# Two pairs of gate/up chunks in each second feed-forward stage computed as seven block products

## The chip, the core and the metric

The kernel runs on one core of a Trainium2 chip. The metric is device time of one execution in microseconds (us). The names of the engines in the profile: PE is TensorE (PEld its weight loads), DVE is VectorE, ACT is ScalarE, POOL is GpSimd, SP issues DMAs. On each engine instructions run in the order in which the program was written; engines wait for each other by semaphores.

## What is computed

A decoder trunk of two layers on 256 tokens of width 1024, in float32. Each layer is a half feed-forward step, a mixer (a state-space group beside differential attention), cross attention to 256 memory tokens, and a second half feed-forward step. Only the feed-forward matters here:

```python
def rms_norm(x, gain):
    y = x32 * lax.rsqrt(jnp.mean(x32 * x32, axis=-1, keepdims=True) + EPS)
    return y * gain
def swiglu(x, w_gate, w_up, w_down):
    return (jax.nn.silu(x @ w_gate) * (x @ w_up)) @ w_down
...
    h = h + 0.5 * swiglu(rms_norm(h, ffn2_norm[l]), ffn2_w_gate[l], ffn2_w_up[l], ffn2_w_down[l])
```

The inner width is 2816, cut into 11 chunks of 256 columns. Gate and up columns of a chunk stand side by side, so a chunk is a product of 256 tokens x 1024 by 1024 x 512.

## The kernel before

**Precision.** Every float32 operand of a matmul is split in two parts: `hi` is a copy rounded to TensorE's fast format (ACT, line 264), `lo` is the remainder (DVE, line 227). A product is three matmuls, hi·hi, hi·lo and lo·hi, added in PSUM. The weights are split on the core as they stream in from memory, so each weight costs one ACT and one DVE pass.

**Units.** All weights stream as units of 128 x 1024 numbers (512 KB), in the order that `stream_plan` writes out. A gate/up unit (kind A) is two blocks of the contraction for the 512 columns of one chunk; a chunk has 4 units. A down unit (kind B) is 128 rows by 1024 columns. One unit serves both blocks of 128 tokens (t = 0 and 1), which is 12 matmuls of 512 columns. In what follows that is called a slot. A feed-forward stage has 44 gate/up slots and 22 down slots.

**A plain chunk.** `project` runs the 4 units of a chunk for both token blocks into two PSUM tiles `mm`. For each block, ACT then takes silu of the gate half (`sg`), DVE multiplies by the up half (`g`), PE transposes `g` into a `tp` bank, and ACT and DVE split the transposed chunk into `gT`. Two chunks later (`LAG`) the two down slots of the chunk add it to the accumulators `acc`.

**The order of the work.** The program keeps a clock of its own (`Clock`) with a cost for every instruction, and uses it only to decide in which order instructions are written to the queues. `tick` is called before each three matmuls, four times in a slot: it first calls `feed`, then lets side tasks write whatever the clock says is due (`run_due`), and adds 0.64 us to the planned position `main`. Each unit has a planned position `need`. `feed` writes the split of a unit when its `need` is at most 4.0 us (`LEAD`) ahead of `main`, which is six ticks, one and a half slots, and when one of five buffers (`N_W`) is free. So an evacuation that a side task writes at the end of a slot stands in DVE's queue ahead of the splits for everything that is more than one and a half slots away.

**Gains.** The gain vector of the norm in front of a stage is multiplied into the weights, as the scale of the two split instructions (`split_unit`, halves of 512 columns). The row factor of the norm is applied at the evacuation.

**Seams.** `prep` adds a stage's result to the residual `h`, transposes it and splits it into `xh`, `xl` for the next stage; the first chunk of the next stage runs all of t = 0 before t = 1, to give t = 1 the time.

**Tables.** `ssm_tables(1)`, which prepares constants of layer 1's mixer, runs as a side task during layer 0's second feed-forward stage.

Of the kernel before, what the change touches and what calls it, by code (L numbers as in the profile page):

```python
# [11 lines left out]
F32 = mybir.dt.float32  # L12
# [7 lines left out]
L = 2  # L20
D = 1024
# [24 lines left out]
START = (22.0, 34.0)  # L46


def rel_bucket(n):
# [26 lines left out]
def stream_plan():  # L76

    plan = []
    for l in range(L):
        def ffn(nm):  # L80
            for j in range(NCH):
                for kp in range(4):
                    plan.append((nm + "_gu", l, 4 * j + kp, "A", (nm, l, 2 * kp), 4 if j == 0 and len(plan) >= 4 else 1))
                if j >= LAG:
                    for f in range(2):
                        plan.append((nm + "_dn", l, 2 * (j - LAG) + f, "B", None, 1))
            for n in range(2 * (NCH - LAG), 2 * NCH):
                plan.append((nm + "_dn", l, n, "B", None, 2 * LAG))

        def chunk(nm, c, norm, skew):  # L90
# [17 lines left out]
        ffn("ffn2")  # L108
# [210 lines left out]
class Trunk:  # L319
    def __init__(self, ctx, tc, io):  # L320
        self.tc, self.io = tc, io
        self.c = Clock(tc.nc)
        self.v, self.a, self.g, self.p = Vector(self.c), Scalar(self.c), Pool(self.c), Tensor(self.c)
        P = lambda name, bufs, **kw: ctx.enter_context(tc.tile_pool(name=name, bufs=bufs, **kw))
        self.const = P("const", 1)
        self.xp = P("xp", 2)
        self.rawp = P("raw", N_RAW)
        self.hip = P("hi", N_W)
        self.lop = P("lo", N_W)
        self.tab = P("tab", 1)  # L330
# [9 lines left out]
        self.tp = P("tp", 2, space=bass.MemoryType.PSUM)  # L340
# [4 lines left out]
        self.raw, self.w = {}, {}  # L345
# [14 lines left out]
        return self.sm.tile([128, n], F32, tag=f"{name}{n}", name=name)  # L360

    def tpt(self):
        p = self.tp.tile([128, 512], F32, tag="tp", name="tp")
        self.tpown[id(p)] = (p, len(self.tpfree))
        self.tpfree.append(math.inf)
        return p

    def tp_done(self, p):
# [1 line left out]

    def tp_wait(self):

        while self.tpfree[-2] + TPW > self.c.now:
            yield max(self.c.now + 0.01, min(self.tpfree[-2] + TPW, self.c.now + 0.3))

    def mmt(self):
        c = self.c
# [37 lines left out]
    def split(self, hi, lo, src):  # L415
        self.a.activation(hi, src, AF.Copy)
        self.v.tensor_tensor(lo, src, hi.bitcast(F32), op=ALU.subtract)

    def rstd(self, r, ssq, n, wd):
        self.g.tensor_scalar(r, ssq, 1.0 / wd, EPS, op0=ALU.mult, op1=ALU.add)  # L420
        self.g.tensor_tensor(r, r, self.mhalf[:, 0:n], op=ALU.pow)
# [16 lines left out]
    def feed(self, least=-1):  # L438

        c = self.c  # L440
        prev, c.cur = c.cur, self.stream
        n = len(self.plan)
        while self.nsplit < 2 * n:
            u, q = divmod(self.nsplit, 2)
            if u >= self.nfree + N_W or (u > least and self.need[u] + q * STEP / 2 > self.main + LEAD):
                break
            self.split_next()
        c.cur = prev

    def split_next(self):  # L450
        u, q = divmod(self.nsplit, 2)
        self.load_to(u + 1)
        self.split_unit(u, q)
        self.nsplit += 1
        self.load_to(u + N_RAW + q)

    def load_to(self, m):
        while self.nload < min(m, len(self.plan)):
            r = self.rawp.tile([128, 1024], F32, tag="raw", name="raw")
            self.tc.nc.sync.dma_start(r, self.io["wst"][self.nload])  # L460
            self.raw[self.nload] = r
            self.nload += 1

    def split_unit(self, i, q):
        kind, gain = self.plan[i][3:5]
# [186 lines left out]
        return out  # L652


    def prep(self, t, acc, coef):
        h = self.h[t]
        t0 = []
        for n in range(2):
            s = slice(512 * n, 512 * n + 512)
            self.v.scalar_tensor_tensor(h[:, s], acc[n], coef, h[:, s], op0=ALU.mult, op1=ALU.add)  # L660
            t0.append(self.c.cur.t)
        self.acc_done()
        x = self.xt()
        for n in range(2):
            self.c.cur.t = t0[n]
            yield
            yield from self.tp_wait()
            p = self.transpose4(h, [512 * n + 128 * i for i in range(4)])
            o = [a[:, 4 * n:4 * n + 4, :].rearrange("p a b -> p (a b)") for a in x]
            self.split(o[0], o[1], p)  # L670
            self.tp_done(p)
        self.x[t] = x
        with self.c.aside():
            self.row_stat(t)
# [56 lines left out]
    def ffn(self, nm, preps, tail):  # L731
# [53 lines left out]
                    self.free_unit()  # L785
        for i in range(NCH - LAG, NCH):
            self.c.wait(*tasks[i])
        base = NCH - LAG
        return self.blocks(nm + "_dn", accs, lambda t, k: xs(base + k // 2, k % 2, t), 2 * LAG, False, True, tail)

# [651 lines left out]
    def setup(self):  # L1442
# [7 lines left out]
        self.nload = 2  # L1450
# [80 lines left out]
    def run(self):  # L1531
        c = self.c
        self.setup()
        preps = None
        prep = lambda coef: (lambda t, acc: self.prep(t, acc, coef))
        tb = {}
        tables = [c.spawn(self.ssm_tables(0, tb), START[0]), c.spawn(self.setup_rest(), START[1])]
        for l in range(L):
            preps = self.ffn("ffn1", preps, prep(0.5))
            preps = self.mixer(l, preps, tb, tables, prep(1.0))  # L1540
            preps = self.cross(l, preps, prep(1.0))
# [6 lines left out]
            preps = self.ffn("ffn2", preps, prep(0.5) if l < L - 1 else (lambda t, acc: self.final(t, acc, 0.5)))  # L1548
        c.wait(*preps)
        c.drain()  # L1550
        assert self.upos == len(self.plan) == self.nfree
# [9 lines left out]
def lay_out(a):  # L1561
# [11 lines left out]
    for l in range(L):  # L1573
# [11 lines left out]
    wst = np.concatenate([groups[s, l][n:n + 1] for s, l, n, _, _, _ in stream_plan()[0]], axis=0)  # L1585
    col = lambda v: v.reshape(-1, 128).T
    gains = np.concatenate(
        [col(f[k][l]) for l in range(L)
# [30 lines left out]
```

## Time and profile before

| what | value |
|---|---|
| median of 3 runs | 1214.55 us (1214.17 to 1214.58) |
| the profiled execution | 1216.16 us, of which the span shown is 1214.3 us |
| PE busy | 1198.7 us (99%) |
| DVE busy | 831.3 us (68%) |
| ACT busy | 701.5 us (58%) |
| granted TensorE clock | 0.999 of full speed |
| second feed-forward of layer 0 | 422.6 to 619.8 us of the span |
| second feed-forward of layer 1 | 1020.3 us to the end |

The profile gives busy time of each engine, the same in 40 slices, the chain of waits that ended last, and groups of like instructions with their number, busy time, mean duration, and the idle time in front of them with what ended it. A view of waits lists who waited for whom, in total, in number, and the longest. The timeline lists instructions in order: start, length, engine, line, operation, output<-inputs, and in brackets the idle time before. Matmuls overlap, so their cost is read from one start to the next.

### The profile page before, as it was taken

Reading aid. Unit: us, or ns where it says so; the run is one execution under the profiler, and the core shown is the slowest. Engines: PE = TensorE matmul, PEld = TensorE weight load, DVE = VectorE, ACT = ScalarE, POOL = GpSimd, SP = SyncE. Lnnn points to the kernel's source line nnn. Section 1 sums busy time; section 2 is a strip of 40 time slices with the busy share of each in tenths; the row PEclk is TensorE's granted clock in tenths of the full one; section 3 lists DMA queues with packets and bytes.
Section 4 is the critical chain, followed back from the end, with each engine's and each line's share of the span. In section 5 each row is a group of like instructions: output and inputs, shape, how many; then the busy total and the mean of one; then the engine's idle time right before and its main releaser. Section 6 shows DMA issues by size and latency. Waiting matters only on the chain.

```text
span 1214.3 us, 17886 instructions
## 1 busy us (share of the span) xinstructions
PE 1198.7 (99%) x6628; PEld 979.9 (81%) x6628; DVE 831.3 (68%) x1502; ACT 701.5 (58%) x1270; POOL 45.1 (4%) x104
## 2 busy tenths in 40 slices
PE   9999999999999999999999999999999999999997
PEld 7888878777888888887888888887678888888886
DVE  5797777497767668777665655565977675655564
ACT  6665455667767555644565554465686665644553
POOL 2100001000000010000100000000000000000000
PEclk9999999999999999999999999999999999999999
DMA  8656556544644465655656555555346445655652
GB/s 281 214 181 191 163 163 188 155 138 123 208 156 138 144 209 184 190 157 158 187 176 218 169 180 192 191 168 162 122 140 209 138 146 166 199 182 191 208 181 79
DMA packets 59975, 210.92 MB, mean 174 GB/s; under 512 B 7168, under 2 KB 8288, under 8 KB 59888
## 3 DMA queue, kind: packets, MB, share of 16 engines
q1 hardware_dynamic: 56304, 202.92, 52.2%
q0 software_dynamic: 2000, 5.24, 1.5%
q10 hardware_dynamic: 1584, 1.62, 0.5%
q8 instruction: 52, 0.85, 0.3%
q14 instruction: 35, 0.29, 0.1%
HBM read 207.00 MB, written 1.05 MB: 171 GB/s over the span
## 4 chain that ended last, share of the span: by engine, by line
PE 93%; DVE 2%; ACT 2%; DMA 1%; issue 1%; ACTq 0%; POOLq 0%; POOL 0%; DVEq 0%
PE mm L303 54%; PE acc L303 32%; PE tp L314 5%; PE tp L303 1%; DMA uq<-z 1%; DVE wlo L227 1%; DVE p L227 1%; ACT junk L264 0%; DMA h<-in_x 0%; ACT whi L264 0%; ACT z L264 0%; DVE nm L227 0%; DVE yT L227 0%; ACT yg L264 0%; ACT up L264 0%
## 5 line engine op out<-in xcount | busy, mean ns | idle before, releaser
L227 DVE SCALAR_TENSOR_TENSOR wlo<-raw,gains,whi 128x512 fp32r<-128x512 f32 x544 | 383.8, 746 | 96.9 <-ACT whi L264 92.5
L264 ACT ACTIVATE whi<-raw,gains 128x512 fp32r<-128x512 f32 x544 | 353.7, 713 | 14.2 <-DMA raw<-in_wst 7.0
L303 PE MATMUL mm<-whi,xh 128*128 128x512 f32 x896 | 356.5, 398 | 0.0
L303 PE MATMUL mm<-whi,xl 128*128 128x512 f32 x896 | 349.8, 390 | 0.0
L303 PE MATMUL mm<-wlo,xh 128*128 128x512 f32 x896 | 349.3, 390 | 0.3 <-DVE wlo L227 0.3
L303 PE MATMUL acc<-whi,gT 128*128 128x512 f32 (+1 forms) x712 | 239.7, 399 | 0.0
L303 PEld LDWEIGHTS mm<-whi,xh 128*128 128x128 f32 x896 | 168.6, 188 | 36.3 <-issue 1.3
L303 PEld LDWEIGHTS mm<-whi,xl 128*128 128x128 f32 x896 | 168.5, 188 | 35.6
L303 PEld LDWEIGHTS mm<-wlo,xh 128*128 128x128 f32 x896 | 168.8, 188 | 33.0 <-DVE wlo L227 0.6
L227 DVE TENSOR_TENSOR wlo<-raw,whi 128x512 fp32r<-128x512 f32 x224 | 147.3, 686 | 37.3 <-ACT whi L264 35.7
L264 ACT ACTIVATE whi<-raw 128x512 fp32r<-128x512 f32 x224 | 130.6, 624 | 59.8 <-DMA raw<-in_wst 42.7
L303 PEld LDWEIGHTS acc<-whi,gT 128*128 128x128 f32 x712 | 133.3, 188 | 25.8
L264 ACT ACTIVATE sg<-mm,rstd 128x256 f32<-128x256 f32 x88 | 41.8, 475 | 190.3 <-PE mm L303 190.1
L303 PE MATMUL acc<-wlo,gT 128*128 128x512 f32 (+1 forms) x356 | 138.2, 388 | 0.0
L227 DVE SCALAR_TENSOR_TENSOR g<-mm,rstd,sg 128x256 f32<-128x256 f32 x88 | 42.4, 482 | 129.0 <-ACT sg L264 128.5
L303 PE MATMUL mm<-whi,mem 128*128 128x512 f32 x256 | 92.6, 410 | 0.0
L303 PEld LDWEIGHTS acc<-wlo,gT 128*128 128x128 f32 x356 | 67.2, 189 | 11.0
L264 ACT ACTIVATE xh<-tp 128x512 fp32r<-128x512 f32 x40 | 23.9, 598 | 77.8 <-PE tp L314 77.8
L303 PEld LDWEIGHTS mm<-whi,mem 128*128 128x128 f32 x256 | 48.1, 188 | 11.5 <-issue 1.3
L303 PE MATMUL mm<-wlo,mem 128*128 128x512 f32 x128 | 51.0, 398 | 3.5 <-DVE wlo L227 3.5
L227 DVE TENSOR_TENSOR xl<-tp,xh 128x512 fp32r<-128x512 f32 x40 | 27.6, 689 | 31.7 <-ACT xh L264 31.7
L264 ACT ACTIVATE gT<-tp 128x512 fp32r<-128x512 f32 x44 | 26.3, 599 | 36.7 <-PE tp L314 36.7
(214 smaller groups left out, 1093.6 us busy)
## 6 DMA issues: line engine op xcount, KB each, us to landing
raw<-in_wst SPq DMA_DIRECT2D x382, 512.0 KB, 4.2
raw<-in_wst SPq DMA_DIRECT2D x4, 256.0 KB, 5.1
mem<-in_mem POOLq DMA_DIRECT2D x2, 512.0 KB, 6.3
uq<-z ACTq DMA_DIRECT2D x8, 128.0 KB, 4.8
bglu<-in_b_glu POOLq DMA_DIRECT2D x2, 512.0 KB, 3.8
h<-in_x SPq DMA_DIRECT2D x3, 256.0 KB, 5.7
bc<-in_s5b POOLq DMA_DIRECT2D x2, 256.0 KB, 3.0
bc<-in_s5c POOLq DMA_DIRECT2D x2, 256.0 KB, 3.1
```

The source lines that it names most:

```text
L227: r = getattr(self.e, name)(*a, **k)
L264: r = self.e.activation(out, in_, func, **k)
L303: r = self.e.matmul(out, lhsT, rhs, **k)
L314: r = self.e.transpose(out, in_, ident)
```

## The change

Chunks 2 and 3, and chunks 7 and 8, of both second feed-forward stages are each computed as a 2 x 2 block product with seven block products instead of eight (Strassen's scheme in Winograd's form). The blocks of the left side are two token blocks by two halves of the contraction, those of the right side two halves of the contraction by two chunks. A block product (`block`) is 2 units of 6 matmuls each into one `tp` bank, one slot in all. Each pair of chunks takes seven such steps.

- The left side: `combos` adds `xh` and `xl` back together, forms four sums of blocks on DVE and splits these once per stage.
- The right side: four weight blocks of 2 units each are loaded, X, Y, P and Q. A step's operand is split when it is due; four of the seven steps first add another block to it on DVE (`split_whole`: add, then ACT's `hi`, then DVE's `lo`, for each of the 2 units).
- The results: three products are copied out by ACT; `sums`, `c11`, `c12` and `c21` put the four results together on DVE, and silu, multiplication, transposition and the split to `gT` follow as before.
- The order of the stage is written out in `SECOND`: P and D are slots of plain gate/up chunks and of down units, S2 and S7 are steps of the two pairs. For reference the slots behind P0 and P1 (eight slots) are numbered 1 to 52 in the order of that string, so that pair 2's seven steps are slots 1, 5, 8, 12, 15, 19, 22 and pair 7's are 26, 29, 33, 36, 40, 43, 46. The steps that add are the third, fourth, sixth and seventh of each pair.
- In these stages the gain is multiplied into `xh` and `xl` at the seam (`split_gain`, four pieces of 128 columns instead of one of 512), and a plain weight unit is split in one piece of 1024 columns instead of two of 512.
- The two `tp` banks are handed out by which is free first instead of in turn, and `ssm_tables(1)` moves to the first feed-forward stage of layer 1.

```diff
+SECOND = (
+    "P0 P0 P0 P0 P1 P1 P1 P1 "
+    "S2 P4 D0 P4 S2 D0 P4 S2 P4 D1 P5 S2 D1 P5 S2 P5 D4 P5 S2 D4 P6 S2 P6 D5 P6 "
+    "S7 D3 P6 S7 D3 D5 P9 S7 P9 D2 S7 D2 P9 D6 S7 P9 D6 S7 P10 P10 S7 P10 P10 D8 D8 D7 D7"
+)
+PAIR = (
+    ("Q3", (1, 1), "X", "X", None),
+    ("Q1", (0, 0), "P", "P", None),
+    ("Q7", (1, 0), "Y", "X", "Y"),
+    ("Q6", None, None, "X", "P"),
+    ("Q2", (0, 1), "Q", "Q", None),
+    ("Q5", None, None, "Y", "P"),
+    ("Q4", None, None, "X", "Q"),
+)
...
-        at += 2 * STEP * n
+        at += STEP if plan[i][3] == "S" else 2 * STEP * n
...
+    def split_gain(self, x, n, src, nm, l):
...
+        for g, b in zip(gc, blk):
+            self.copy(o[0][:, b], src[:, b], scale=g)
...
+            self.v.scalar_tensor_tensor(o[1][:, b], src[:, b], g, o[0][:, b].bitcast(F32), op0=ALU.mult, op1=ALU.subtract)
...
+    def split_whole(self, i):
...
+        if kind == "S":
+            pair, u, _, operand, add = op
+            r = self.blk[pair, operand, u]
+            if add is not None:
+                self.v.tensor_tensor(r, r, self.blk[pair, add, u], op=ALU.add)
+        else:
+            r = self.raw.pop(i)
+        self.split(hi, lo, r)
...
+        def block(ps, name):
+            xh, xl = E[name]
+            for u in range(2):
+                w = self.unit(nm + "_gu")
+                for i in range(2):
+                    self.tick(w[2 + i])
+                    s = slice(512 * i, 512 * i + 512)
+                    k = 2 * u + i
+                    self.p.matmul(ps, xh[:, k, :], w[0][:, s], start=k == 0, stop=False)
+                    self.p.matmul(ps, xh[:, k, :], w[1][:, s], start=False, stop=False)
+                    self.p.matmul(ps, xl[:, k, :], w[0][:, s], start=False, stop=k == 3)
+                self.free_unit()
...
+            def sums():
+                yield st["q1"]
+                v.tensor_tensor(u2, ps, q1, op=ALU.add)
...
+                v.tensor_tensor(u3, u3, u2, op=ALU.add)
...
+                v.tensor_tensor(q3, q3, u2, op=ALU.subtract)
+            def c11():
+                yield st["u"]
+                v.tensor_tensor(q1, ps, q1, op=ALU.add)
+                self.tp_done(ps)
+                yield
+                swiglu(q1, q1, 0)
+            def c12():
+                yield st["u"]
+                v.scalar_tensor_tensor(u2, ps, -1.0, u3, op0=ALU.mult, op1=ALU.subtract)
+                v.tensor_tensor(q3, q3, ps, op=ALU.subtract)
...
+                swiglu(u2, u2, 1)
+                swiglu(q3, q3, 0)
...
         for l in range(L):
+            if l:
+                tb = {}
+                tables = [c.spawn(self.ssm_tables(l, tb), c.now + 12.0)]
...
-            if l < L - 1:
-                tb = {}
-                tables = [c.spawn(self.ssm_tables(l + 1, tb), c.now + 10.0)]
```

More of the change, by code (lines that the diff above doesn't have):

```diff
@@ L46, with second_items @@
 START = (22.0, 34.0)
+SECOND = (
[3 rows of a table added]
+)
[8 more added lines that the diff above has]
+)
+def second_items():
+    seen = {}
+    for item in SECOND.split():
+        k = seen[item] = seen.get(item, -1) + 1
+        yield item[0], int(item[1:]), k
 def rel_bucket(n):
@@ L88, in ffn, with second @@
                 plan.append((nm + "_dn", l, n, "B", None, 2 * LAG))
+        def second(nm):
+            for kind, j, k in second_items():
+                if kind == "P":
+                    plan.append((nm + "_gu", l, 4 * j + k, "A", None, 4 if j == 0 else 1))
+                elif kind == "D":
+                    plan.append((nm + "_dn", l, 2 * j + k, "B", None, 1))
+                else:
+                    _, block, to, operand, add = PAIR[k]
+                    for u in range(2):
+                        n = None if block is None else 4 * (j + block[0]) + 2 * block[1] + u
+                        plan.append((nm + "_gu", l, n, "S", ((l, j), u, to, operand, add), 1))
+            for n in range(2 * (NCH - LAG), 2 * NCH):
+                plan.append((nm + "_dn", l, n, "B", None, 2 * LAG))
         def chunk(nm, c, norm, skew):
@@ L107, in stream_plan @@
             plan.append(("wo", l, k, "B", None, 4))
-        ffn("ffn2")
+        second("ffn2")
     need, at, i = [], 0.0, 0
@@ L371, in tp_wait, with tp_main @@
     def tp_wait(self):
-        while self.tpfree[-2] + TPW > self.c.now:
-            yield max(self.c.now + 0.01, min(self.tpfree[-2] + TPW, self.c.now + 0.3))
+        while min(self.tpfree) + TPW > self.c.now:
+            yield max(self.c.now + 0.01, min(min(self.tpfree) + TPW, self.c.now + 0.3))
+    def tp_main(self):
+        c = self.c
+        while min(self.tpfree) == math.inf or (c.heap and c.heap[0][0] + TPW <= min(self.tpfree) > c.now + TPW):
+            c.step_idle()
+        return self.tpt()
     def mmt(self):
@@ L417, in split @@
         self.v.tensor_tensor(lo, src, hi.bitcast(F32), op=ALU.subtract)
+    def split_gain(self, x, n, src, nm, l):
+        g0 = l * NGAIN + GOFF[nm] + 4 * n
+        gc = [self.gains[:, g0 + i:g0 + i + 1] for i in range(4)]
+        blk = [slice(128 * i, 128 * i + 128) for i in range(4)]
+        o = [a[:, 4 * n:4 * n + 4, :].rearrange("p a b -> p (a b)") for a in x]
+        for g, b in zip(gc, blk):
+            self.copy(o[0][:, b], src[:, b], scale=g)
+        t = self.c.cur.t
+        self.c.cur.t -= 0.6
+        for g, b in zip(gc, blk):
+            self.v.scalar_tensor_tensor(o[1][:, b], src[:, b], g, o[0][:, b].bitcast(F32), op0=ALU.mult, op1=ALU.subtract)
+        self.c.cur.t = max(self.c.cur.t, t)
     def rstd(self, r, ssq, n, wd):
@@ L652, in blocks, with prep @@
         return out
-    def prep(self, t, acc, coef):
+    def prep(self, t, acc, coef, gain=None):
         h = self.h[t]
@@ L668, in prep @@
             p = self.transpose4(h, [512 * n + 128 * i for i in range(4)])
-            o = [a[:, 4 * n:4 * n + 4, :].rearrange("p a b -> p (a b)") for a in x]
-            self.split(o[0], o[1], p)
+            if gain is not None:
+                self.split_gain(x, n, p, *gain)
+            else:
+                o = [a[:, 4 * n:4 * n + 4, :].rearrange("p a b -> p (a b)") for a in x]
+                self.split(o[0], o[1], p)
             self.tp_done(p)
@@ new lines, in ffn_second, with swiglu, to_columns, parts @@
+    def ffn_second(self, nm, preps, tail):
+        c, v = self.c, self.v
+        gT, bank, accs, tasks = {}, {}, None, {}
+        E = {}
+        def swiglu(ps, o, t):
+            c.cur.t = max(c.cur.t, self.rt[t])
+            self.a.activation(o[:, 0:256], ps[:, 0:256], AF.Silu, scale=self.r[t])
+            v.scalar_tensor_tensor(o[:, 256:512], ps[:, 256:512], self.r[t], o[:, 0:256], op0=ALU.mult, op1=ALU.mult)
+        def to_columns(p, g, t):
+            for f in range(2):
+                o = f * 256 + t * 128
+                self.p.transpose(p[:, o:o + 128], g[:, 256 + f * 128:384 + f * 128], self.ident)
+        def parts(j, p):
+            hl = self.s4t([128, 2, 512], F32R, name="gT")
+            self.split(hl[:, 0, :], hl[:, 1, :], p)
+            self.tp_done(p)
+            gT[j] = hl
+        def evac(j, before):
+            def f(t, ps):
+                if before is not None:
+                    yield before[t]
+                z = self.zp.tile([128, 512], F32, tag="z", name="z")
+                swiglu(ps, z, t)
+                self.mm_done()
+                yield
+                if j not in bank:
+                    yield from self.tp_wait()
+                    bank[j] = self.tpt()
+                    to_columns(bank[j], z, t)
+                else:
+                    to_columns(bank[j], z, t)
+                    parts(j, bank[j])
+            return f
+        def chunk_done(j, g0, g1, *deps):
+            for d in deps:
+                yield d
+            yield from self.tp_wait()
+            p = self.tpt()
+            to_columns(p, g0, 0)
+            to_columns(p, g1, 1)
+            parts(j, p)
+        def block(ps, name):
+            xh, xl = E[name]
+            for u in range(2):
+                w = self.unit(nm + "_gu")
[7 more added lines that the diff above has]
+                self.free_unit()
+        def pair_step(j, k):
+            name = PAIR[k][0]
+            if k == 0:
+                c.wait(combo)
+                st.clear()
+                st["s"] = [self.s4t([128, 2, 512], name="qs") for _ in range(2)]
+            q3, q1, u2, u3 = (x[:, i, :] for x in st["s"] for i in range(2))
+            ps = self.tp_main()
+            block(ps, name)
+            def copied(o):
+                self.copy(o, ps)
+                self.tp_done(ps)
+                return
+                yield
+            def sums():
+                yield st["q1"]
+                v.tensor_tensor(u2, ps, q1, op=ALU.add)
+                self.tp_done(ps)
+                yield st["q7"]
+                v.tensor_tensor(u3, u3, u2, op=ALU.add)
+                yield st["q3"]
+                v.tensor_tensor(q3, q3, u2, op=ALU.subtract)
+            def c11():
+                yield st["u"]
+                v.tensor_tensor(q1, ps, q1, op=ALU.add)
+                self.tp_done(ps)
+                yield
+                swiglu(q1, q1, 0)
[3 more added lines that the diff above has]
+                v.tensor_tensor(q3, q3, ps, op=ALU.subtract)
+                self.tp_done(ps)
+                yield
+                swiglu(u2, u2, 1)
+                swiglu(q3, q3, 0)
+            def c21():
+                yield st["c12"]
+                v.tensor_tensor(u3, ps, u3, op=ALU.add)
+                self.tp_done(ps)
+                yield
+                swiglu(u3, u3, 1)
+            if name == "Q3":
+                st["q3"] = c.spawn(copied(q3))
+            elif name == "Q1":
+                st["q1"] = c.spawn(copied(q1))
+            elif name == "Q7":
+                st["q7"] = c.spawn(copied(u3))
+            elif name == "Q6":
+                st["u"] = c.spawn(sums())
+            elif name == "Q2":
+                st["c11"] = c.spawn(c11())
+            elif name == "Q5":
+                st["c12"] = c.spawn(c12())
+                tasks[j + 1] = [c.spawn(chunk_done(j + 1, q3, u2, st["c12"]))]
+            else:
+                tasks[j] = [c.spawn(chunk_done(j, q1, u3, st["c11"], c.spawn(c21())))]
+        st = {}
+        combo = None
+        def xs(j, f, t):
+            o = f * 256 + t * 128
+            return gT[j][:, 0, o:o + 128], gT[j][:, 1, o:o + 128]
+        before, ps = None, None
+        for kind, j, k in second_items():
+            if kind == "P":
+                if j == 0:
+                    if k == 0:
+                        tasks[0] = self.project(nm + "_gu", self.x, evac(0, None), preps)
+                    if k < 3:
+                        continue
+                    before = tasks[0]
+                    combo = c.spawn(self.combos(E))
+                    continue
+                if k == 0:
+                    ps, tasks[j] = [self.mmt(), self.mmt()], []
+                u = self.unit(nm + "_gu")
+                for t in range(2):
+                    self.mm_a(ps[t], self.x[t], u, 2 * k, k == 0, k == 3)
+                    if k == 3:
+                        tasks[j].append(c.spawn(evac(j, before)(t, ps[t])))
+                self.free_unit()
+                if k == 3:
+                    before = tasks[j]
+            elif kind == "S":
+                pair_step(j, k)
+            else:
+                c.wait(*tasks[j])
+                if accs is None:
+                    accs = [self.acc_main(), self.acc_main()]
+                u = self.unit(nm + "_dn")
+                for t in range(2):
+                    self.mm_b(accs[t], *xs(j, k, t), u, j == 0 and k == 0, False)
+                self.free_unit()
+        for i in range(NCH - LAG, NCH):
+            c.wait(*tasks[i])
```

92 lines of the change are left out of this document (74 added, 18 removed).

## The prediction

> **What bounds the kernel now.** I read the page's first lines, then who TensorE waits for, then the busy time of the feed-forward stages, then TensorE's own pace.
>
> ```profile
> span 1214.3 us, 17886 instructions
> PE 1198.7 (99%) x6628; PEld 979.9 (81%) x6628; DVE 831.3 (68%) x1502; ACT 701.5 (58%) x1270; POOL 45.1 (4%) x104
> ```
>
> The waits of PE (total, times, longest):
>
> ```profile
> PE mm L303 <- DVE wlo L227: 3.8, 5, 1.4
> PE tp L314 <- ACT up L264: 1.9, 2, 1.0
> ```
>
> Three stages: layer 0's second feed-forward, layer 1's first, layer 1's second up to the last split. After the colon pair come length, then busy time of PE, PEld, DVE, ACT, POOL, then the granted clock.
>
> ```profile
> 422.60:619.80 197.20, 197.20 (x1110) 160.91 (x1109) 145.94 (x310) 108.11 (x187) 9.56 (x20) 1.00 0.59 181
> 619.80:806.70 186.90, 186.90 (x854) 153.82 (x853) 111.83 (x174) 99.99 (x174) 1.48 (x4) 1.00 0.56 186
> 1020.30:1206.60 186.30, 186.28 (x857) 153.61 (x855) 111.51 (x175) 99.53 (x173) 1.29 (x3) 1.00 0.53 177
> ```
>
> In these stages PE is never idle. A busy PE need not be at its peak, so I also read its pace:
>
> ```profile
> 463.19 0.39 PE L303 MATMUL mm<-whi,xh 128*128 128x512 f32 x1
> 463.41 0.39 PE L303 MATMUL mm<-wlo,xh 128*128 128x512 f32 x1
> 463.64 0.39 PE L303 MATMUL mm<-whi,xl 128*128 128x512 f32 x1
> 463.87 0.39 PE L303 MATMUL mm<-whi,xh 128*128 128x512 f32 x1
> ```
>
> Four starts span 0.68 us: one matmul per 0.227 us. So the kernel is bound by the number of matmuls, and a removed one gives 0.227 us as long as nothing else becomes late. A slot of 12 takes 2.72 us; with the transposes in it, the stage of 66 slots gives 186.9 / 66 = 2.83 us per slot.
>
> **What is removed.** A pair of chunks takes 8 slots of 12 = 96 matmuls now, and 7 x 12 = 84 after. Twelve less per pair, four pairs: 48 x 0.227 = 10.9 us, 5.45 us per layer. Transposes stay at four per chunk. [...] The trace shows 227 ns here, and 10.9 stands.
>
> **What is added, and on whom.** Durations of the pieces:
>
> ```profile
> L227 DVE SCALAR_TENSOR_TENSOR wlo<-raw,gains,whi 128x512 fp32r<-128x512 f32 x544 | 383.8, 746 | 96.9 <-ACT whi L264 92.5
> L227 DVE TENSOR_TENSOR p<-p 128x1024 f32<-128x1024 f32 x4 | 4.9, 1220 | 0.1
> L264 ACT ACTIVATE up<-uq 128x1024 f32<-128x1024 f32 x2 | 2.1, 1056 | 5.5 <-DMA uq<-z 5.5
> L227 DVE SCALAR_TENSOR_TENSOR g<-mm,rstd,sg 128x256 f32<-128x256 f32 x88 | 42.4, 482 | 129.0 <-ACT sg L264 128.5
> L264 ACT ACTIVATE sg<-mm,rstd 128x256 f32<-128x256 f32 x88 | 41.8, 475 | 190.3 <-PE mm L303 190.1
> L227 DVE TENSOR_TENSOR gT<-tp,gT 128x512 fp32r<-128x512 f32 x44 | 30.3, 690 | 23.8 <-ACT gT L264 23.7
> ```
>
> Two instructions back to back overlap a little:
>
> ```profile
> 521.38 2.35 DVE L227 TENSOR_TENSOR Vt<-pr,bbar 128x1024 f32<-128x1024 f32 x2
> ```
>
> Two of 1.22 us in 2.35: the second starts 1.13 to 1.14 us after the first. So on a busy DVE a pass over 1024 costs 1.14, over 512 0.61 (gT) to 0.60, `g` 0.40.
>
> A plain unit is cheaper than before: one pass of 1.14 on DVE instead of two of 0.75 less the same overlap, and it has no bearing on PE. A step's unit without an add costs the same 1.14, but feeds only 6 matmuls. A unit with an add is the dear one. Its three instructions stand next to each other in the program: DVE adds (1.22), ACT makes `hi` from the sum (1.06), DVE makes `lo` from sum and `hi` (1.14). DVE runs in order, so it stands still while ACT works. What follows an engine starts 0.03 us after it:
>
> ```profile
> 665.18 0.69 DVE L227 TENSOR_TENSOR wlo<-raw,whi 128x512 fp32r<-128x512 f32 x1 [1.13 <-ACT whi L264]
> 670.53 0.48 DVE L227 SCALAR_TENSOR_TENSOR g<-mm,rstd,sg 128x256 f32<-128x256 f32 x1 [4.67 <-ACT sg L264]
> 671.05 0.69 DVE L227 TENSOR_TENSOR wlo<-raw,whi 128x512 fp32r<-128x512 f32 x1
> ```
>
> and on ACT:
>
> ```profile
> 670.03 0.47 ACT L264 ACTIVATE sg<-mm,rstd 128x256 f32<-128x256 f32 x1 [4.88 <-PE mm L303]
> ```
>
> ACT ends at 670.50, DVE starts at 670.53. So one such unit holds DVE for 1.22 + 0.03 + 1.06 + 0.03 + 1.14 = 3.48 us, a step of two units for 6.96, while the step itself takes PE 2.72. There are four such steps in each pair.
>
> These rows show a second thing. DVE stood idle for 4.67 us in front of `g`, with weights left to split: `g` waits for PE's last matmul of the chunk, and the splits behind it in the queue wait too. The planner writes a split six ticks, 1.5 slots, before its use; so whatever is due later than 1.5 slots after such an evacuation can only begin after it. This is how I find the due dates: start from an evacuation that waits for PE, add up DVE's queue from there to the last `lo` of a step, and compare with PE's time to the middle of that step (1.36 us into it, when its second unit starts). Numbers are slots.
>
> *Step 22 (the last of the first pair).* The result of step 15 is evacuated by `c11`, 0.2 us after slot 15 ends (a matmul's 0.39 less 0.227, and the hop). DVE then has: `c11` 0.60, its `g` 0.40, unit 18 1.14, step 19 6.96, unit 20 1.14, two `g` of chunk 5 0.80, unit 21 1.14, `gT` 0.61, the two of `c12` 1.20, step 22 6.96. With the 0.2: 21.15 us. PE gets there in 6 x 2.83 + 1.36 = 18.3. Late by 2.8 us.
>
> *Step 46 (the last of the second pair).* From the end of slot 40: 0.2, `c11` and `g` 1.00, step 43 6.96, two `g` of chunk 9 0.80, unit 44 1.14, `gT` 0.61, unit 45 1.14, `c12` 1.20, step 46 6.96: 20.0 us. PE needs 5 x 2.83 + 1.36 = 15.5. Late by 4.5 us, part of it already at step 43.
>
> *Step 12.* From the end of slot 9, where chunk 4 ends: 0.2, silu 0.50, `g` 0.40, step 12 6.96 = 8.06, with chunk 4's `gT` before its second unit 8.67. PE needs 2 x 2.83 + 1.36 = 7.0. Late by 1.05 to 1.65; I take 1.3.
>
> *Steps 8, 19, 33, 36* come out in time the same way. Step 19: 0.2 + 1.00 + 1.14 + 6.96 = 9.3 of 9.85. Step 36, from the end of slot 28: 0.2 + 0.9 + 0.61 + 4 x 1.14 + 2 x 6.96 = 20.2 of 21.2. In front of step 8 no DVE instruction waits for PE.
>
> *Slot 1.* In the four slots of P1 DVE gets the block sums: two of 1.14, four of 0.60, the first split (0.60 on ACT, then 0.61), besides four units (4.56), a `gT` (0.61) and the evacuation (1.1): 12.2 us against 12.7 to the middle of slot 1. If the other three splits (1.2 each) come ahead it is up to 3 late. I take 0.5, with 0 and 3 as ends.
>
> Per layer 2.8 + 4.5 + 1.3 + 0.5 = 9.1 us of waits, 18.2 in both.
>
> **The rest, at nothing.** At the seam `xh` and `xl` are made in four pieces of 128 columns:
>
> ```profile
> 428.46 0.60 ACT L264 ACTIVATE xh<-tp 128x512 fp32r<-128x512 f32 x1 [0.53 <-PE tp L314]
> 429.09 0.69 DVE L227 TENSOR_TENSOR xl<-tp,xh 128x512 fp32r<-128x512 f32 x1 [0.43 <-ACT xh L264]
> L264 ACT ACTIVATE sb<-sb,nm 128x128 f32<-128x128 f32 x16 | 6.2, 392 | 4.5 <-DVE nm L227 4.4
> L227 DVE SCALAR_TENSOR_TENSOR sb<-sb,sums 128x128 f32<-128x128 f32 x8 | 2.8, 351 | 0.3
> ```
>
> Four of these take about 4 x 0.3 = 1.2 us instead of 0.6 to 0.7, so the second half of t = 1 is ready at some 430.4 instead of 429.8. PE begins t = 1 at 428.95 and wants that half 12 matmuls later, at 431.7. The matmuls of t = 0 cover it; without cover it would be 0.6 us per half. The tables of layer 1 move with all their instructions, their DMAs on POOL's queue too, from the 197.2 us stage to the 186.9 us one: 34 us of DVE into a stage where it has 75 to spare, exactly what the other stage bore without a wait of PE, and the 10 us that they cost PE move along. SP's queue carries 8 loads per pair as before; the steps without a load leave it idle. Of the `tp` banks a step holds one for about 2.7 + 0.8 us, a chunk's transposes the other for two to three, and steps are two slots apart at least: 0, and if a bank is late, below 1 us each time.
>
> **The sum.** The profiled execution took 1216.16 us (its span 1214.3); the runs' median is 1214.55, and what changes adds to either. -10.9 + 18.2 = +7.3: 1221.9 us by the runs. Ends of this case: without the `gT` and one `g` in front, and nothing at slot 1, the waits are 1.8 + 3.5 + 1.05 = 6.35 per layer, +1.8, 1216.4; with `c12`'s two `g` in front of the last unit (0.80 in two places), 1.65 at step 12 and 3 at slot 1 they are 3.6 + 5.3 + 1.65 + 3.0 = 13.55, +16.2, 1230.8.
>
> **Rivals.**
> *DVE's standstill is filled.* If the 1.12 us between add and `lo` hold other due DVE work, or adds run ahead of the evacuations, a step costs 4.56 or less. Step 22 is in time once 0.7 of the 1.12 are filled in its four units, step 46 only when nearly all is; then the 10.9 us stay: 1203.7, or 1204 to 1212 when part does. For it: in the 197.2 us stage DVE was busy for 145.9 and PE still did not wait; and a pair's adds and splits alone are busy for 22 x 1.14 = 25.1 us of the 18 slots (51 us) about it. Against it: add, `hi` and `lo` are written one after the other, and the row at 670.53 shows that nothing overtakes.
> *The waits eat just the gain.* With 4.2 to 6.7 us of waits per layer the result is within 0.2% (2.4 us, about what a measurement can tell): around 1214.5.
> *The clock falls.* The trace opens with TensorE at half pace:
>
> ```profile
> 7.65 0.63 PE L303 MATMUL mm<-whi,xh 128*128 128x512 f32 x1
> 8.08 0.63 PE L303 MATMUL mm<-whi,xl 128*128 128x512 f32 x1
> 8.51 0.63 PE L303 MATMUL mm<-whi,xh 128*128 128x512 f32 x1
> 10.06 0.40 PE L303 MATMUL mm<-whi,xh 128*128 128x512 f32 x1
> 10.30 0.39 PE L303 MATMUL mm<-wlo,xh 128*128 128x512 f32 x1
> ```
>
> It takes 0.43 us per matmul for over 2 us of work, then 0.227. A long wait could bring that state back: 1 us for the 2.2 us seen here, some 4 if the whole slow opening of 9 us counts. With the long waits at steps 22 and 46 in two layers that is 4 to 16 us on top, 1226 to 1238. Against it: before, no wait of 1.4 us did so, and each lateness here is shared by two units with 6 matmuls between. [...]
>
> **Chances.** Forecast 0.54, from the queue's order, which I trust more than its exact sums; standstill filled in good part 0.32, since a queue that runs ahead at some steps would undo the larger terms; even 0.08; clock 0.06. So faster 0.32, same 0.08, slower 0.60. The likeliest case alone spans 1216 to 1231; to hold 8 in 10 the range must take in most of the faster case: 1205 to 1230, which leaves out a full saving and the clock's fall.
>
> **What would show it.** In the profile after: 48 matmuls fewer, at 0.227 us still; among the waits of PE, its step matmuls on DVE's `lo`, some 18 us in all, the longest in steps 22 and 46; on DVE, `lo` of the steps waiting about 1.1 us each for ACT, 32 times. If PE's waits stay below 8 us in all, the due dates are wrong and the change is faster. If PE waits as long but for transposes or banks, the place is wrong.

## The result and the profile after

The changed kernel takes 1235.72 us (median of 4 runs, 1232.87 to 1238.97) against 1214.55 before (also 4 runs): ratio 1.0172, 95% interval 1.0155 to 1.0189. It is slower, as forecast, but by 21.2 us instead of 7.3, and outside the range. The profiled execution took 1238.06 us, its span 1236.3. Lines of `before.py` 227, 264 and 303 are lines 268, 305 and 344 of this kernel.

The first lines of the page, and then the waits of PE (total, times, longest):

```profile
span 1236.3 us, 17726 instructions
PE 1201.5 (97%) x6580; PEld 973.4 (79%) x6580; DVE 904.8 (73%) x1498; ACT 711.1 (58%) x1206; POOL 45.1 (4%) x104
```

```profile
PE tp L344 <- DVE wlo L268: 10.7, 16, 0.8
PE tp L344 <- ACT whi L305: 4.7, 8, 0.9
PE mm L344 <- DVE wlo L268: 4.1, 5, 1.4
PE tp L344 <- ACT eh L305: 2.4, 2, 1.2
```

48 matmuls are gone (6628 to 6580). The 4.1 us that `mm` waits for `wlo` was there before (3.8). New are the waits of `tp`, the bank of the step products, for the splits of the step's weights and of the block sums (`eh`). The three stages again:

```profile
421.90:617.90 196.00, 186.24 (x829) 148.94 (x829) 148.41 (x168) 105.87 (x139) 1.48 (x4) 1.00 0.51 176
617.90:815.00 197.10, 197.10 (x1109) 160.83 (x1108) 146.10 (x310) 106.61 (x186) 9.58 (x20) 1.00 0.58 181
1029.20:1228.60 199.40, 189.77 (x833) 151.93 (x831) 148.25 (x170) 103.99 (x137) 1.90 (x4) 0.97 0.49 164
```

The middle row now carries the tables: 197.1 us, just what the stage that had them took before (197.2), so the move is neutral. A feed-forward stage without tables took 186.9 us before; with 24 matmuls fewer it should take 181.5. The second one of layer 0 takes 196.0, and PE, which had no holes there, is now busy for 186.2 of them.

Where they lie follows from the starts of the matmuls: for each slot, the time from its first start to the next slot's, less 12 x 0.227 and 0.109 per transpose.

| late by (us) | forecast | layer 0 | layer 1 |
|---|---|---|---|
| slot 1 and the transposes ahead of it | 0.5 | 2.98 | 2.94 |
| step 12 | 1.3 | 1.59 | 1.54 |
| step 22 | 2.8 | 3.41 | 5.89 |
| steps 33 and 36 | 0 | 1.75 | 1.73 |
| steps 43 and 46 | 4.5 | 5.08 | 6.59 |
| all | 9.1 | 14.8 | 18.7 |

DVE in front of step 22 of layer 0, in its order, shows the queue that the prediction added up, instruction for instruction (`qs` at 491.69 is `c11`, the two at 504 are `c12`):

```profile
491.69 0.69 DVE L268 TENSOR_TENSOR qs<-tp,qs 128x512 f32<-128x512 f32 x1 [1.11 <-PE tp L344]
492.30 1.22 DVE L268 TENSOR_TENSOR wlo<-raw,whi 128x1024 fp32r<-128x1024 f32 x1
493.44 0.48 DVE L268 SCALAR_TENSOR_TENSOR qs<-qs,rstd 128x256 f32<-128x256 f32 x1
493.83 1.22 DVE L268 TENSOR_TENSOR blkY<-blkY,blkP 128x1024 f32<-128x1024 f32 x1
496.25 1.23 DVE L268 TENSOR_TENSOR wlo<-blkY,whi 128x1024 fp32r<-128x1024 f32 x1 [1.21 <-ACT whi L305]
497.40 1.22 DVE L268 TENSOR_TENSOR blkY<-blkY,blkP 128x1024 f32<-128x1024 f32 x1
499.83 1.23 DVE L268 TENSOR_TENSOR wlo<-blkY,whi 128x1024 fp32r<-128x1024 f32 x1 [1.21 <-ACT whi L305]
...
504.02 0.69 DVE L268 SCALAR_TENSOR_TENSOR qs<-tp,qs 128x512 f32<-128x512 f32 x1
504.62 0.68 DVE L268 TENSOR_TENSOR qs<-qs,tp 128x512 f32<-128x512 f32 x1
505.22 0.68 DVE L268 TENSOR_TENSOR gT<-tp,gT 128x512 fp32r<-128x512 f32 x1
505.82 1.22 DVE L268 TENSOR_TENSOR blkX<-blkX,blkQ 128x1024 f32<-128x1024 f32 x1
508.22 1.23 DVE L268 TENSOR_TENSOR wlo<-blkX,whi 128x1024 fp32r<-128x1024 f32 x1 [1.19 <-ACT whi L305]
```

The bracket in front of each such `wlo` is the standstill: 1.2 us in which DVE waits for ACT's `hi` of the sum that DVE has just made. PE at the same place:

```profile
508.31 0.43 PE L344 MATMUL tp<-whi,xh 128*128 128x512 f32 x1
509.50 0.51 PE L344 MATMUL tp<-wlo,xh 128*128 128x512 f32 x1 [0.76 <-DVE wlo L268]
...
511.79 0.50 PE L344 MATMUL tp<-whi,xh 128*128 128x512 f32 x1 [0.87 <-ACT whi L305]
513.05 0.50 PE L344 MATMUL tp<-wlo,xh 128*128 128x512 f32 x1 [0.76 <-DVE wlo L268]
```

From start to start it loses 0.96 us once and 1.03 twice. Layer 1 has the same waits, and a second loss: in step 22 and step 46 the granted clock falls to half. The window before the fall and the fall itself (third to last column: the clock), then the same at step 46:

```profile
1115.66:1119.07 3.41, 1.81 (x8) 0.96 (x6) 2.23 (x3) 1.21 (x2) 0.00 (x0) 1.00 0.00 0
1119.07:1125.90 6.83, 6.30 (x16) 4.67 (x17) 5.82 (x8) 4.42 (x7) 0.00 (x0) 0.50 0.67 241
1194.17:1197.58 3.41, 1.79 (x7) 0.93 (x6) 2.23 (x5) 3.24 (x5) 0.00 (x0) 1.00 0.00 0
1197.58:1200.99 3.41, 3.41 (x12) 2.72 (x11) 3.11 (x4) 2.05 (x3) 0.00 (x0) 0.50 0.41 94
```

In the first of the two rows with 0.50 matmuls start 0.43 us apart (1124.24, 1124.66, 1125.09) instead of 0.227. The two last 10.24 us, which at half pace costs up to 5.1.

### The profile page after: what moved, and what is told of

Its sections match the earlier page's. It is cut to its first block, busy times and chain, and to the rows that moved or that the text cites. A ratio compares the mean times of both kernels' runs of the same rounds, so it can differ in the third digit from the quotient of the medians.

```text
span 1236.3 us, 17726 instructions
## 1 busy us (share of the span) xinstructions
PE 1201.5 (97%) x6580; PEld 973.4 (79%) x6580; DVE 904.8 (73%) x1498; ACT 711.1 (58%) x1206; POOL 45.1 (4%) x104
## 4 chain that ended last, share of the span: by engine, by line
PE 81%; DVE 11%; ACT 4%; issue 2%; DMA 1%; ACTq 0%; POOLq 0%; POOL 0%; DVEq 0%
PE mm L344 42%; PE acc L344 29%; PE tp L344 6%; PE tp L355 5%; DVE wlo L268 5%; ACT whi L305 3%; DVE blkX L268 2%; DMA uq<-z 1%; DVE blkY L268 1%; DVE qs L268 1%; DVE p L268 1%; DVE gT L268 1%; DMA h<-in_x 0%; DVE z L268 0%; DVE xf L268 0%
## 5 line engine op out<-in xcount | busy, mean ns | idle before, releaser
L268 DVE SCALAR_TENSOR_TENSOR wlo<-raw,gains,whi 128x512 fp32r<-128x512 f32 x368 | 263.1, 747 | 92.9 <-ACT whi L305 91.5
L344 PE MATMUL mm<-whi,xh 128*128 128x512 f32 x768 | 308.0, 401 | 0.0
L344 PE MATMUL mm<-wlo,xh 128*128 128x512 f32 x768 | 300.6, 392 | 0.3 <-DVE wlo L268 0.3
L344 PE MATMUL mm<-whi,xl 128*128 128x512 f32 x768 | 300.8, 392 | 0.0
L305 ACT ACTIVATE whi<-raw,gains 128x512 fp32r<-128x512 f32 x368 | 240.9, 713 | 14.3 <-DMA raw<-in_wst 5.7
L268 DVE TENSOR_TENSOR wlo<-raw,whi 128x512 fp32r<-128x512 f32 (+1 forms) x236 | 209.0, 912 | 29.0 <-ACT whi L305 27.9
L305 ACT ACTIVATE whi<-raw 128x512 fp32r<-128x512 f32 (+1 forms) x236 | 181.0, 805 | 45.6 <-DMA raw<-in_wst 18.9
L305 ACT ACTIVATE whi<-blkX 128x1024 fp32r<-128x1024 f32 x32 | 33.6, 1057 | 55.0 <-DVE blkX L268 55.0
L268 DVE TENSOR_TENSOR wlo<-blkX,whi 128x1024 fp32r<-128x1024 f32 x32 | 39.2, 1225 | 33.7 <-ACT whi L305 33.7
L305 ACT ACTIVATE z<-mm,rstd 128x256 f32<-128x256 f32 (+1 forms) x52 | 29.4, 568 | 39.5 <-PE mm L344 38.9
```

Of the source, the lines that this page charges most:

```text
L268: r = getattr(self.e, name)(*a, **k)
L305: r = self.e.activation(out, in_, func, **k)
L344: r = self.e.matmul(out, lhsT, rhs, **k)
```

## The experiments

State of the question: the theory is that DVE's standstill between add and `lo` makes the queues of the steps too long (with the block sums late at slot 1 as a second cause). Rivals: the sheer amount of work on DVE and ACT, the planner's short lead, the block steps or the other edits themselves.

**Adds together.** The second add fills the time in which ACT makes the first `hi`:

```diff
-            if add is not None:
-                self.v.tensor_tensor(r, r, self.blk[pair, add, u], op=ALU.add)
+            if add is not None and u == 0:
+                for k in range(2):
+                    a = self.blk[pair, operand, k]
+                    self.v.tensor_tensor(a, a, self.blk[pair, add, k], op=ALU.add)
```

> Edit: the two adds of a step stand together ahead of its two splits, so that DVE makes the second add while ACT makes the first hi. Nothing is left out. Standstill theory (DVE waits about 1.1 us for ACT in each of the 32 units with an add): a step holds DVE for about 1.22 + 1.14 + 0.0 + 1.14 + 1.14 = 4.65 us instead of 6.96. By the slots of the changed kernel's profile PE waits 14.7 us per layer: 3.0 at slot 1, 1.6 at step 12, 3.4 at step 22, 1.7 at steps 33 and 36, 5.1 at steps 43 and 46. Two steps lie in the stretch that ends at 22 and in the one that ends at 46, so 4.6 us are taken from each: what stays is 3.0 at slot 1 and some 0.5 at step 46, and the time is 1214.55 - 10.9 + 7.0 = 1210.7, with 1208 to 1214. Rival, the amount of work on DVE and ACT (adds and double splits) is the limit and not its order: nothing changes, about 1233. Rival, the planner's lead of 1.5 slots is the limit: below 2 us gained, about 1231.

Measured: 1213.66 us (11 runs), ratio to before 0.9992 (0.9983 to 1.0). 22 us of the changed kernel's time are gone with the same instructions in another order: the standstill theory holds, the amount of work as the limit falls. What is late is slot 1 by 4.1 to 4.2 us in each layer (a fall of the clock in it each time), step 22 by 0.7, step 46 by 0.2, nothing else. That is 3 us above the sum; the falls at slot 1 take up to 3.4 of it.

**No adds.**

```diff
-            if add is not None:
-                self.v.tensor_tensor(r, r, self.blk[pair, add, u], op=ALU.add)
```

> Edit: the 32 adds of weight blocks are left out (the steps multiply blocks that are not summed, so the feed-forward is not the reference's); all splits, steps and evacuations stay. Standstill theory: no unit holds DVE for more than 1.14 us, only slot 1's 3.0 us per layer stay: 1214.55 - 10.9 + 6.0 = 1209.7, with 1208 to 1212. Rival, the block steps themselves cost time (banks of PSUM, units of 6 matmuls, results put together on DVE): above 1220. Rival, the amount of DVE work: the time lies between this and 1233 in proportion to the 32 x 1.14 = 36 us taken from DVE, well above the kernel with the adds together, which keeps them.

Measured: 1211.9 us (9 runs), 0.9972 (0.9963 to 0.9982). Only 1.8 us less than with the adds together: of the 24 us that the 32 adds cost in the changed kernel, falls of the clock included, 22 are their place in the queue and 2 their work. Nothing is late but slot 1.

**All plain.** Plain chunks and down units alone, no block sums:

```diff
-SECOND = (
...
+SECOND = "P0 P0 P0 P0 P1 P1 P1 P1 P2 P2 P2 P2 D0 D0 P3 P3 P3 P3 D1 D1 ... P10 P10 P10 P10 D8 D8"
...
-                    combo = c.spawn(self.combos(E))
```

> Edit: the order of the second stages is all plain chunks, no pair and no block sums; the gain at the seam, splits in one piece, free choice of the transpose banks and the moved tables stay. Prediction's reading (all these at nothing): 1214.5, within 1. Rival, part of the loss is theirs (seam, bank choice, tables in the other stage): 1216 or more.

Measured: 1215.48 us (11 runs) beside 1214.71 before on that chip, ratio of the runs 1.0003 (0.9994 to 1.0012): no difference that can be told. The gain at the seam, whole splits, bank choice and moved tables together cost nothing that can be told (1.5 us at most, by the interval).

**First step later.**

```diff
-    "S2 P4 D0 P4 S2 D0 P4 S2 P4 D1 P5 S2 D1 P5 S2 P5 D4 P5 S2 D4 P6 S2 P6 D5 P6 "
+    "D0 P4 S2 D0 P4 S2 P4 P4 S2 D1 P5 S2 D1 P5 S2 P5 D4 P5 S2 D4 P6 S2 P6 D5 P6 "
```

> Edit: in the order of the first pair two plain slots (D0 P4) are moved from between its first steps to the front of it, so that the first step comes at slot 3; the number of slots is the same. Theory of the block sums (they reach the first step 3.0 us late in each layer because DVE is full through the four slots ahead): 5 to 6 us gained, about 1227.5, with 1226 to 1230. Rival, the wait in front of slot 1 is PE's for the transposes of chunk 1 and stays wherever the first step stands: 1231 to 1234.

Measured: 1236.84 us (4 runs), 1.0177 (1.0163 to 1.0192). A miss in the time, not in the place: slot 1 is on time in both layers (below 0.15 us), but step 12 is late by 4.0 (with a fall of the clock in it) and 2.4 instead of 1.6, and the profile has the clock at half for 3.4 to 6.8 us five times ahead of the run's end instead of twice. What was gained in front was lost behind, mostly to the clock: the five falls last 20.5 us, which costs up to 10.2. The profile's span less that is 1235.4 - 10.2 = 1225.2; for the changed kernel the same sum gives 1230 to 1231 (its second profile stands at the end of this section). By this estimate the 5 to 6 us are there, and the falls take them.

**Both.** The first and the last of these edits:

```diff
-    "S2 P4 D0 P4 S2 D0 P4 S2 P4 D1 P5 S2 D1 P5 S2 P5 D4 P5 S2 D4 P6 S2 P6 D5 P6 "
+    "D0 P4 S2 D0 P4 S2 P4 P4 S2 D1 P5 S2 D1 P5 S2 P5 D4 P5 S2 D4 P6 S2 P6 D5 P6 "
...
+            if add is not None and u == 0:
+                for k in range(2):
```

> Edit: both the adds of a step together and the first step at slot 3. Standstill and block sums together explain the loss: of the waits per layer about 1 us stays (0.7 at step 22, 0.2 at step 46, a little at step 12), so 1214.55 - 10.9 + 2 = 1205.7, with 1204.5 to 1208; with no long wait left the granted clock falls at most at the end of the run, and the runs lie within 1.5 us of each other. Rival, the moved slots only shift the wait (as with the first step at slot 3 alone, where the time did not change): 1211 to 1214.

Measured: 1206.0 us (5 runs, 1205.48 to 1207.77), 0.9932 (0.992 to 0.9944). This beats both kernels, by 8.5 us the one before, of the 10.9 that the matmuls are worth. First lines of its page, waits of PE, and DVE at one of its steps:

```profile
span 1204.2 us, 17722 instructions
PE 1187.3 (99%) x6580; PEld 969.4 (81%) x6580; DVE 904.3 (75%) x1498; ACT 712.8 (59%) x1206; POOL 45.2 (4%) x104
```

```profile
PE mm L344 <- DVE wlo L268: 4.2, 5, 1.4
...
PE tp L344 <- DVE wlo L268: 0.9, 2, 0.5
```

```profile
488.32 2.35 DVE L268 TENSOR_TENSOR blkY<-blkY,blkP 128x1024 f32<-128x1024 f32 x2
490.75 2.36 DVE L268 TENSOR_TENSOR wlo<-blkY,whi 128x1024 fp32r<-128x1024 f32 x2
```

Two adds and two `lo` hold DVE for 4.8 us without a bracket, and DVE's busy time is that of the changed kernel (904.3 and 904.8 us). Per layer 0.7 us at step 22 and 0.2 at step 46 stay, and the clock stays whole up to the last 5 us of the span. The wait at slot 1 is shown by this pair of kernels: with the adds together, moving the first step is worth 7.7 us, of which the two falls at slot 1 can take up to 3.4.

**Longer lead.**

```diff
-LEAD = 4.0
+LEAD = 6.6
```

> Edit: the planner's lead is 6.6 us instead of 4.0, that is ten ticks or 2.5 slots instead of 1.5, with adds and splits as in the changed kernel. Order theory (a split due later than the lead stands behind an evacuation that waits for PE; the standstill makes the stretch behind it too long): both units of steps 22 and 46 now stand ahead of c12 and its gT, unit 18 and step 43 ahead of c11, step 12 ahead of chunk 4's evacuation. By the same sums step 22 needs 18.2 of 18.3 us, step 46 25.2 of 26.8 counted from the end of slot 36, so only slot 1's 3 us and one or two more per layer stay: 1210 to 1216. Rival, DVE simply has too much to do with 32 standstills in it, whatever the order: 1226 to 1233.

Measured: 1260.81 us (4 runs), 1.0382 (1.0368 to 1.0396). The order theory as I put it falls. Steps 12, 33, 36 and 43 are in time, as the sums had it, and no matmul of step 22 waits for a split any more: the 2.5 and 1.6 us that it still loses are falls of the clock. But PE now waits at slots 0 and 1 (7.4 and 6.6 us, falls included), ahead of step 22 (3.1, for DVE's evacuation `qs` of the bank) and ahead of step 46 (2.0, for `gT`). The clock is at half for 44.4 us ahead of the end, which costs up to 22 of the 46 us lost. And the second stage of layer 0 begins 11 us later than in the changed kernel: the longer lead harms the stages before it as well.

**Longer lead in the second stages only.**

```diff
-            if u >= self.nfree + N_W or (u > least and self.need[u] + q * STEP / 2 > self.main + LEAD):
+            if u >= self.nfree + N_W or (u > least and self.need[u] + q * STEP / 2 > self.main + (6.6 if self.plan[u][0].startswith("ffn2") else LEAD)):
```

> Edit: the planner's lead of 6.6 us applies to the units of the second stages alone; the other stages keep 4.0. With the lead longer everywhere the first of these stages took 200 us, some 3.5 of them half-clock loss for each 6.8 us window, and the rest of the kernel was 20 us longer. If DVE with its standstills is full whatever the order, the second stages keep 11 to 13 us of waits per layer, moved from the splits to evacuations and transposes, and the time is 1227 to 1235. If the order was the limit and the longer lead hurt the other stages alone: 1210 to 1218.

Measured: 1240.38 us (4 runs), 1.0211 (1.0194 to 1.0228): not better than the changed kernel, and 5 us above the upper end that I gave, with six half-clock windows of 3.4 us in its profile. The waits of PE there:

```profile
PE tp L344 <- ACT eh L305: 6.8, 2, 3.4
PE tp L344 <- DVE qs L268: 5.9, 2, 2.9
...
PE tp L344 <- DVE gT L268: 3.9, 2, 2.1
```

Splits written earlier stand in front of evacuations and block sums, and these are late instead. The six falls last 20.5 us and cost up to 10.2; 1237.9 - 10.2 = 1227.7 in span is only 2 to 4 us below the changed kernel without its falls. With the standstills in the queue, earlier splits mostly choose which product waits.

**Together in the first pair only.** As in the first experiment, for the pair of chunks 2 and 3 alone:

```diff
-            if add is not None:
-                self.v.tensor_tensor(r, r, self.blk[pair, add, u], op=ALU.add)
+            for k in range(2):
+                if add is not None and (k == u if pair[1] != 2 else u == 0):
+                    a = self.blk[pair, operand, k]
+                    self.v.tensor_tensor(a, a, self.blk[pair, add, k], op=ALU.add)
```

> Edit: the two adds of a step stand together in the first pair of each stage alone; the second pair keeps add, hi, lo per unit. Standstill theory, step by step: the first pair's waits (1.6 at step 12, 3.4 at step 22, less some 0.7 that stay) go, 4.3 per layer, the second pair's (0.5, 1.2, 1.8, 3.3) stay as they are: 8.6 less than the changed kernel, 1223 to 1229 with the falls of the clock that the long wait at step 46 still brings. Rival, the waits of one pair are handed on to the other: the second pair's waits change by more than 1 us per layer.

Measured: 1228.18 us (4 runs), 1.0106 (1.0091 to 1.0121). Step 12 is in time, step 22 late by 0.67; steps 33, 36 and 43 keep 0.53, 1.2 and 1.8 us to a few hundredths, and step 46 keeps its 3.1, with a fall of 3.4 us behind it in each layer. The waits belong to their own pair and are not handed on.

**Adds on POOL**, with the first step later:

```diff
-                self.v.tensor_tensor(r, r, self.blk[pair, add, u], op=ALU.add)
+                self.g.tensor_tensor(r, r, self.blk[pair, add, u], op=ALU.add)
```

> Edit: the 32 adds are made by POOL instead of DVE, with the first step at slot 3. Standstill theory: DVE no longer stands between add and lo, and POOL, idle here, adds as soon as the blocks have landed: 1205 to 1207. Rival, POOL's reads slow DVE down or its add takes longer than the lead: 1208 to 1220.

Measured: 1233.49 us (4 runs, 1227.79 to 1235.27), 1.016 (1.0145 to 1.0176), a miss. POOL's adds and DVE's splits beside them:

```profile
464.89 6.63 POOL L328 TENSOR_TENSOR blkX<-blkX,blkP 128x1024 f32<-128x1024 f32 x2 [6.85 <-DVE wlo L268]
```

```profile
465.87 3.42 DVE L268 TENSOR_TENSOR wlo<-raw,whi 128x1024 fp32r<-128x1024 f32 x1
```

An add takes 3.3 us there, and DVE's 1.22 us pass takes 3.42 beside it: DVE is slowed, as the rival had it, at more than its price; whether POOL's reads do it is not shown. The profiled execution (1227.79) has no fall ahead of its end, and its span of 1225.6 is that of the first step later alone, less its falls (1225.2). So the standstill is gone, and DVE is slower by about as much.

**The changed kernel again**, without an edit.

> The changed kernel once more, unedited, for the spread of its runs beside the others on this chip. If the granted clock falls to half after long waits in some executions and not in others, the runs scatter in steps of about 1.7 us (half of a 3.4 us window) between some 1231 and 1240. Rival, the scatter is of another origin: no relation between the number of half-clock windows in the profile and the time.

Measured: 1237.58 us (4 runs, 1235.52 to 1239.05), 1.0188 (1.0174 to 1.0202). Its profile has the clock at half for 3.4, 6.8 and 3.4 us ahead of the end, at slot 1 and steps 22 and 46 of layer 0, where the first profile had it at steps 22 and 46 of layer 1. The span less half of these is 1237.0 - 6.8 = 1230.2; for the first profile 1236.3 - 5.1 = 1231.2. So the same kernel without a fall would be at some 1231 in span, 1233 in time, where the two shortest of its runs lie. The record has the mean granted clock of every run: 0.997 and 0.998 in those two (1232.87 and 1233.38 us), 0.997 and 0.995 at 1235.52 and 1236.35, 0.993 to 0.994 in the four from 1238.06 to 1239.05. The kernel with both edits, which has no fall ahead of its end, has 0.998. If each of the eight runs is given back what its clock lacks to that (0.001 is 1.24 us), their spans, 1231.1 to 1237.3, come to lie within 1229.9 and 1232.5. So most of the scatter is the falls', and the rival of another origin is left with little.

## Why the prediction was wrong in size

**Right.** PE's pace and the 10.9 us (with both edits 8.5 are gained, and 1.8 still go in waits). The tables, the seam and the rest at nothing (the all-plain kernel). The standstill, its 3.48 us per unit (from 493.83 to 497.40 it is 3.57), the order of DVE's queue, and the due dates at step 12 (1.3 forecast, 1.6 measured), step 22 (2.8, 3.2 to 3.4) and steps 43 and 46 (4.5, 5.1). The signs named for it came: 48 matmuls fewer, `tp` waiting for `wlo`, 1.2 us of standstill before each `lo` of a sum.

**Wrong: "I take 0.5" at slot 1.** It was 3.0, the upper end, in each layer; this is the largest of the misses. The sum of DVE's work ended with the first split of the block sums. In the trace DVE is busy without a hole from 434.77 to 447.0, but unit 2's split, chunk 1's two `g` and its `gT` stand ahead of that first split:

```profile
443.78 1.22 DVE L268 TENSOR_TENSOR wlo<-raw,whi 128x1024 fp32r<-128x1024 f32 x1
444.92 0.69 DVE L268 SCALAR_TENSOR_TENSOR ef<-ef,xf 128x512 f32<-128x512 f32 x1
445.52 0.87 DVE L268 SCALAR_TENSOR_TENSOR z<-mm,rstd,z 128x256 f32<-128x256 f32 x2
446.31 0.68 DVE L268 TENSOR_TENSOR ef<-xf,ef 128x512 f32<-128x512 f32 x1
447.55 0.69 DVE L268 TENSOR_TENSOR gT<-tp,gT 128x512 fp32r<-128x512 f32 x1 [0.56 <-ACT gT L305]
448.16 2.49 DVE L268 TENSOR_TENSOR el<-ef,eh 128x512 fp32r<-128x512 f32 x4
```

The last block sum comes at 446.31, when PE has been through with P1 for over a microsecond. I had listed what the step needs, not what the queue holds. The due date was wrong as well. ACT's splits of the block sums, and then PE with chunk 1's transposes and the first matmul of the step:

```profile
447.41 2.18 ACT L305 ACTIVATE eh<-ef 128x512 fp32r<-128x512 f32 x4
```

```profile
446.06 0.83 PE L355 MATMUL tp<-ident,z 128*128 128x128 f32 x4 [0.70 <-DVE z L268]
448.09 0.50 PE L344 MATMUL tp<-whi,eh 128*128 128x512 f32 x1 [1.20 <-ACT eh L305]
```

The first matmul already reads `eh`. So the first split is due at the start of slot 1 and not in its middle, 1.36 us earlier, and against the 11.3 us to there the same 12.2 are 0.9 late before anything is added to the list.

**Wrong: "Steps 8, 19, 33, 36 come out in time".** 33 and 36 were late by 1.75 together. The due dates counted evacuations on DVE as the points where a queue waits for PE; ACT has such points too. The copy of step 29's product stands in ACT's queue ahead of the `hi` of unit 32, and DVE's `lo` waits for it:

```profile
535.06 0.60 ACT L305 ACTIVATE qs<-tp 128x512 f32<-128x512 f32 x1 [0.78 <-PE tp L344]
535.55 1.05 ACT L305 ACTIVATE whi<-raw 128x1024 fp32r<-128x1024 f32 x1
```

```profile
536.64 1.23 DVE L268 TENSOR_TENSOR wlo<-raw,whi 128x1024 fp32r<-128x1024 f32 x1 [1.49 <-ACT whi L305]
```

From 537.8 DVE then runs through both steps without any hole but the standstills, and is late at both.

**Wrong: "clock 0.06".** The fall was named as a rival, priced at 1 to 4 us each, and set aside because no earlier wait of 1.4 us brought one and each wait is shared by two units with matmuls between. Falls came in both profiles of the kernel, 5 and 7 us in price, 1.7 or 3.4 each. The trace of the kernel before has a fall too, at its end: its granted clock is 0.50 from 1211.4 us on, from 4.8 us after PE's last matmul. The falls in the first profile of the changed kernel last 3.41 and 6.83 us, and PE was not idle in the window before them: it was busy for 1.8 of 3.41 us.

**The account.** Forecast -10.9 + 18.2. Without falls the waits are 14.7 per layer by the table (layer 1's larger values hold the falls): -10.9 + 29.4 = +18.5, or 1233.1. The falls bring the median to 1235.7. Of the 11.2 us by which the waits came out longer than forecast, slot 1 has 5.0 and steps 33 and 36 have 3.5; the rest lies at steps 12, 22, 43 and 46, which were right in place and short in size. The sign was no luck: the standstill that gave it is the one whose removal took the loss away. The rival of a filled standstill (0.32) did not happen in this kernel; when the adds were put together it did, and the loss went as that rival had it.

## What to carry to other kernels

In an in-order queue an operation that goes to another engine and back costs the round trip, not its own length (here 3.57 us per unit, in which DVE is busy for 2.45); count it as occupied time, and look whether a sibling of the same step can stand in the gap. When summing a queue up to a due date, list all that is written ahead on every engine of the chain, with each point where one of them waits for the bound engine. Before a scheme that saves the bound engine one part in eight is dropped for being slower, look where it waits: here two edits of order turned a loss of 21 us into a gain of 8.5.

## What the runs showed of the hardware

- In the changed kernel the granted clock fell to half, for 3.4 or 6.8 us, after 3.41 us windows in which PE was busy for 1.5 to 1.8 us with waits of about 1 us between matmuls. The same waits in the other layer of the same run did not always bring it. In its first profile the falls start at 1119.07, 1197.58 and, at the end of the run, 1231.71 us, which is 23 and 10 times 3.413 us apart. These are its windows of that grid at step 22 and step 46 of layer 0, with 2.06 and 1.95 us of PE busy, after which the clock stayed whole:

```profile
508.09:511.50 3.41, 2.06 (x8) 1.05 (x6) 2.36 (x2) 0.93 (x2) 0.00 (x0) 1.00 0.00 0
583.18:586.59 3.41, 1.95 (x6) 1.05 (x6) 2.23 (x3) 2.00 (x4) 0.00 (x0) 1.00 0.00 0
```

  In both profiles of the changed kernel and in the runs with adds together, no adds, first step later, lead in the second stages, and first pair only, a fall came after each window of such a grid, ahead of the end, with at most 1.82 us of PE busy (21 of them), and after none with 1.90 or more. PE's busy time alone does not tell when one comes: the longer lead and the adds on POOL have eight windows of 1.49 to 1.77 us without a fall. In the kernel with 0.9 us of waits per layer there was none ahead of the end.
- A POOL add of two blocks of 128x1024 in float32 took 3.1 to 3.4 us on average by group, and DVE's two-operand pass of 1.22 us took up to 3.42 beside it. The pass is a plain one with two operands in float32. What slows it is not shown by these runs.
